# Moving the activation tiles by 192 bytes, and cutting 512-column products into halves, in a one-layer hybrid decoder kernel

## The chip, the cores and the metric

The kernel runs on one core of one Trainium2 chip. The metric is the time of one execution on the device in microseconds (us). Three runs of the kernel before gave 962.97, 963.48 and 963.52 us; the median, 963.48 us, is what the changed kernel is held against.

## The reference

One layer of a decoder trunk in float32, on 512 positions of width 1024. What matters here is the list of matrix products and what stands between them:

```
h    = rmsnorm(x, norm_mix_g)
proj = h @ w_in                          # 1024 x 9232
bg, cg, xv, q, k, v, z, a, b, ga, gb = split(proj)
y_a  = (bg * causal_dwconv(cg * xv, conv_a_w)) @ w_a_out
y_b  = gdn_branch(q, k, v, z, a, b, ...) @ w_b_out   # chunked gated delta rule
mix  = sigmoid(ga) * y_a + sigmoid(gb) * y_b
x    = x + mix @ w_o
h    = rmsnorm(x, norm_ffn_g)
gate, val = split(causal_dwconv(h @ w_up, ffn_conv_w))   # 2 x 2816
x    = x + (silu(gate) * val) @ w_down
out  = rmsnorm(x, norm_final_g)
```

## The kernel before

**Products.** Activations are held transposed: 128 channels of a block on the partitions, the 512 positions in the free dimension. Every float32 operand is split into a rounded part and a remainder (`wh`, `wl` for weights, two tiles for activations), and a product of two of them is three TensorE products with rounded operands, all issued by the helper `mm` (line 108 of the profile). In a product one operand streams through the array (the moving one, 512 or 256 columns of it), the other is loaded into it beforehand by a weight load (the stationary one, 128 columns). Each product here has a weight load of its own.

**Jobs.** The program is a list of jobs, and each takes a block of weights (four quarter tiles `wh` and four `wl`, from 12 buffers of each). A *plain job* (`col_job`) makes 256 output channels: two banks, 24 products of 512 columns into each, 48 in all. A *sum job* (`sum_job`) makes the same output by a Strassen-like scheme from 84 products of 256 columns: 12 on a quarter of the activations, 48 on sums of quarters (tiles `ts` for the first norm's output `hT`, `us` for the second's, `h2`), and 24 on two more quarters. In both the weights are stationary and the activations move. In the `w_o` and `w_down` jobs the roles are exchanged: tiles `mix`, `mixb`, `xs` are stationary, and `wh`, `wl` move, 512 columns nearly always.

**Stages.** To about 29 us: the first norm and the first K job, partly by an order written out by hand (`manual_schedule`). Then 19 plain jobs on `hT` (Q, V, Z, K of four head pairs, and the gate GB), and between their products the small float32 products of the delta rule (to about 314 us). Then 16 jobs for CG, XV, BG and GA (ten sum jobs, six plain), four plain jobs each on `yas` and `yb`, the `w_o` jobs on `mix` and `mixb` (to about 613 us), the second norm, the 22 jobs of `w_up` (eight sum jobs on `h2` and `us`; two blocks at the start that already go by halves of 256 columns, lines 1440 to 1460; twelve plain), and the `w_down` jobs on `xs`.

**What sets the order.** `mm` counts columns, and after every `SLAB * S` = 2048 of them (four products of 512 columns, or eight of 256) it calls `tick`, which advances the side work by a step: the delta rule's chains, the evacuation of a finished bank (`evacs`, always only the task at the head of the queue), the splitting of the next block of weights (`splits`: `act.copy` line 140, `dve.tensor_tensor` line 141). On top of the order in which the program issues things, the framework's scheduler places instructions on each engine by its own costs, outside the hand-ordered stretches. A finished bank of a Q, K or V job goes through `conv` in a tile `cv` (three buffers) and a Silu (line 973).

**Where tiles lie.** The addresses are fixed when the program is built. Per partition, modulo 256 bytes, the tiles start at:

| tile | before | after | start minus that of `wh`, before | after |
|---|---|---|---|---|
| `wh`, `wl`, `raw` | 32 | 224 | 0 | 0 |
| `hT`, `h2` | 32 | 160 | 0 | 192 |
| `ts`, `us` | 224 | 160 | 192 | 192 |
| `yas` | 96 | 224 | 64 | 0 |
| `yb` | 32 | 224 | 0 | 0 |
| `mix`, `mixb`, `xs` | 224 | 224 | 192 | 0 |

All slices of them that a product reads start a multiple of 256 bytes further. Below, the fourth and fifth columns are called the *offset* of an operand pair. The small float32 products of the delta rule read tiles that all move by the same amount, so their offsets stay.

Of the kernel before, what the change touches and what calls it, by code (L numbers as in the profile page):

```python
# [9 lines left out]
F32 = mybir.dt.float32  # L10
F32R = mybir.dt.float32r
# [5 lines left out]
P = 128  # L17
S = 512
NT = S // P
D = 1024  # L20
ND = D // P
# [39 lines left out]
def layer_kernel(ctx, tc, x, norm_mix_g, w_in, w_ab, conv_a_w, gdn_conv_w, gdn_A_log, gdn_dt_bias,  # L61
# [14 lines left out]
    def nm(s):  # L76
        cnt[0] += 1
        return f"{s}{cnt[0]}"
# [137 lines left out]
            use(block.wh, block.wl)  # L216


    gate = const.tile([1, 16], F32, name="gate")

    def feed(raw):
        el = raw[0:1, 1].rearrange("p k n -> p (k n)") if len(raw.shape) == 4 else raw[0:1, 1]
# [8 lines left out]
    def products(o, wh, wl, j, x_, lo=0, hi=S, order=KO):  # L231
        mm3(o[:, lo:hi], [(piece(wh, j, k), piece(wl, j, k), x_[0][:, k, lo:hi], x_[1][:, k, lo:hi])
                          for k in order])

    def col_job(w, i, xs, consume, pre=None):
        def use(wh, wl):
            if pre:
                pre()
            x_ = xs() if callable(xs) else xs
            for j in range(GW // P):  # L240
                o = bank()
                products(o, wh, wl, j, x_)
                evacs.append(Task(consume(j, o)))
        return Block(lambda: w[i]), use

# [24 lines left out]
    def sum_job(w, i, xs, sums, consume, place, pre=None):  # L270
# [56 lines left out]
            evacs.append(Task(last()))  # L327
        return SumBlock(lambda: w[i]), use

    def split(dst, idx, src):  # L330
        act.copy(out=dst[0][:, idx], in_=src)
        dve.tensor_tensor(out=dst[1][:, idx], in0=src, in1=dst[0][:, idx].bitcast(F32), op=ALU.subtract)
# [26 lines left out]

    p1 = ExitStack()  # L360
    hp = p1.enter_context(tc.tile_pool(name="hp", bufs=1))
    hT = [hp.tile([P, ND, S], F32R, tag=f"h{i}", name=f"hT{i}") for i in range(2)]
    yb = hp.tile([P, ND, S], F32, name="yb")


# [15 lines left out]
    HS = S // 2  # L381
# [227 lines left out]
    Dms = {}  # L609

    def gates_chain(o):
        abT = gd.tile([P, S], F32, tag="cv", bufs=3, name="abT")[0:32]
        act.copy(out=abT, in_=o[0:32, :])
        yield
        o2 = bank()
# [342 lines left out]
    def pair_jobs(pr):  # L958
        st = {}

        def qkv(which, j, o):
            c = gd.tile([P, S], F32, tag="cv", bufs=3, name=nm("cv"))
            yield from conv(c, o, gdn_w(which * 8 + 2 * pr + j), 4)
            if which == 1 and j == 0:
                reach(pr - 2, 99)
                st["kq"] = gd.tile([P, 2, 2, S], F32, tag="kq", bufs=2, name=nm("kq"))
                st["kqs"] = hp.tile([P, 2, 2, 2, S], F32R, tag="s", name=nm("kqs"))
            if which == 2 and j == 0:
                if pr:
                    ftask[pr - 1].until(VREAD)  # L970
                st["vT"] = gd.tile([P, 2, S], F32, tag="vT", name=nm("vT"))
            dst = (lambda: st["kq"][:, j, 1, :], lambda: st["kq"][:, j, 0, :], lambda: st["vT"][:, j, :])[which]()
            act.activation(out=dst, in_=c, func=AF.Silu)
            yield
            if which < 2:
                hi, lo = (st["kqs"][:, i, j, 1 - which, :] for i in range(2))
                act.copy(out=hi, in_=dst)
                dve.tensor_tensor(out=lo, in0=dst, in1=hi.bitcast(F32), op=ALU.subtract)
                yield
            if which == 2 and j == 1:  # L980
                st["v"] = True
            if which == 0 and j == 1:
                ftask[pr] = Task(front(pr, st))
                chains.append(ftask[pr])

        def zc(j, o):
            act.activation(out=yb[:, 2 * pr + j, :], in_=o, func=AF.Silu)
            if j == 1:
                st["z"] = True
            yield  # L990

        def first_k(wh, wl):
            use_ab()
            for j in range(2):
                products(o_k[j], wh, wl, j, hT, HS, S)
                evacs.append(Task(qkv(1, j, o_k[j])))

        return [(k_block, first_k) if pr == 0 else col_job(w_in, C_K + pr, hT, lambda j, o: qkv(1, j, o)),
                col_job(w_in, C_Q + pr, hT, lambda j, o: qkv(0, j, o)),
                col_job(w_in, C_V + pr, hT, lambda j, o: qkv(2, j, o)),  # L1000
                col_job(w_in, C_Z + pr, hT, zc)]
# [21 lines left out]
    st = {}  # L1023
# [52 lines left out]
    def open_conv():  # L1076
        drain(evacs)
        drain(chains)
        drain(mids)
        drain(backs)  # L1080
        p2.close()
        sc = st["sc"] = p3.enter_context(tc.tile_pool(name="sc", bufs=1, side="right"))
        st["ts"] = [place(i, "ts").rearrange("p (m a n) -> p m a n", m=4, a=4) for i in range(2)]
        st["ya"] = sc.tile([P, ND, S], F32, name="ya")
        room["pool"] = sc
        adds.extend((Task(o_w.form()), Task(down_w.form())))
        sums_of.append(Task(activation_sums(hT, st["ts"], sc.tile([P, ND, S], F32, tag="mixa", name="xf"))))


    def place(i, name, up=0):  # L1090
        return st["sc"].tile([P, ND * S + 64], F32R, tag=f"t{i}", name=f"{name}{i}")[:, up:up + ND * S]

    def open_mix():
        st["mixa"] = st["sc"].tile([P, ND, S], F32, tag="mixa", name="mixa")
# [65 lines left out]
        return c  # L1160

    def split_ya():
        st["yas"] = [place(i, "yas", 32).rearrange("p (k n) -> p k n", k=ND) for i in range(2)]
        for k in range(ND):
            split(st["yas"], k, st["ya"][:, k, :])
            yield

    def split_yb():
        st["yb"] = [hp.tile([P, ND, S], F32R, tag=f"h{i}", name=f"yb{i}") for i in range(2)]
        for k in range(ND):  # L1170
            split(st["yb"], k, yb[:, k, :])
            yield
# [18 lines left out]
    def wb_c(g):  # L1191
        def c(j, o):
            m = 2 * g + j
            t, mix = tmp("t"), st["mixa"][:, m, :]
            dve.tensor_tensor(out=t, in0=o, in1=sgb[0][:, m, :], op=ALU.mult)
            dve.tensor_tensor(out=mix, in0=t, in1=mix, op=ALU.add)
            yield
            if j == 1 and g % 2 == 1:
                if g == 1:
                    st["mix"] = [place(i, "mix").rearrange("p (m a n) -> p m a n", m=4, a=4) for i in range(2)]  # L1200
                yield from prep_a(mix_pairs(g - 1), st["mix"], g - 1)
        return c

# [93 lines left out]
    def open_o():  # L1297
# [2 lines left out]
        fp = ctx.enter_context(tc.tile_pool(name="fp", bufs=1))  # L1300
        st["x1"] = fp.tile([P, NT, D], F32, name="x1")
        st["fp"] = fp
        st["h2"] = [fp.tile([P, ND, S], F32R, tag=f"h2{i}", name=f"h2{i}") for i in range(2)]
        s7 = st["s7"] = p7.enter_context(tc.tile_pool(name="s7", bufs=2))
        gff = st["gff"] = s7.tile([P, D], F32, name="gff", bufs=1)
        nc.sync.dma_start(out=gff, in_=norm_ffn_g[0].partition_broadcast(P))
# [85 lines left out]
    def open_up():  # L1392
# [2 lines left out]
        up = st["up"] = ctx.enter_context(tc.tile_pool(name="up", bufs=1, side="right"))  # L1395
        cvp = st["cvp"] = ctx.enter_context(tc.tile_pool(name="cvp", bufs=2))
        room["pool"], room["o"] = cvp, 2
        st["ts"] = [up.tile([P, 4, 4, HS], F32R, tag=f"t{i}", name=f"us{i}") for i in range(2)]
        st["aT"] = [up.tile([P, NA, S], F32, name="aTa")]
        xf = up.tile([P, ND, S], F32, tag="late", name="xf2")  # L1400
        st["gfn"] = cvp.tile([P, D], F32, name="gfn", bufs=1)
# [66 lines left out]

    def xs():
        if "xs" not in st:  # L1470
            st["xs"] = [st["up"].tile([P, 4, 4, HS], F32R, tag=f"t{e}", name=f"xs{e}") for e in range(2)]
        return st["xs"]

    def ffn_pairs(g, n):
# [206 lines left out]
```

## Time and profile before

| what | value |
|---|---|
| median of three runs | 963.48 us |
| the profiled execution's own time | 963.13 us |
| its span, first to last instruction | 961.4 us |
| TensorE (PE) busy | 950.7 us, 99% |
| VectorE (DVE) busy | 743.9 us, 77% |
| ScalarE (ACT) busy | 507.6 us, 53% |
| DMA | 138.11 MB, mean 144 GB/s |
| granted TensorE clock | 0.998 |

A row of the timeline gives the start of a run of like instructions, the time to the end of its last one, engine, line, operation, `out<-in` by tile names, and the number merged into the row. Matmuls are pipelined: the next starts long before the one before it has ended, so the *spacing*, from start to start, is what a product costs, and not its duration.

### The profile page before, as it was taken

The page shows a single profiled execution, that of the slowest core. Times are in us where ns is not written, and L with a number is a line of the kernel's source. Part 1 is how long each engine was busy: PE and PEld are TensorE (multiplying, and loading weights), DVE is VectorE, ACT ScalarE, POOL GpSimd, SP SyncE. Part 2 cuts the span into 40 slices and gives each one's busy share as a digit, 9 for nine tenths or more (in the row PEclk, how much of TensorE's full clock was granted, in tenths as well). Part 3 has the DMA queues.
Part 4 walks back from the last instruction along what each step waited for, and adds up shares of the span by engine and source line. Part 5 has one row for each costly group of instructions (what it writes and reads, how often), then busy time and mean ns, then how long its engine had stood idle before and what let it go on. Part 6 is the DMA issues. An engine that isn't in the chain of part 4 may idle for free.

```text
span 961.4 us, 16188 instructions
## 1 busy us (share of the span) xinstructions
PE 950.7 (99%) x6188; PEld 823.1 (86%) x6188; DVE 743.9 (77%) x1401; ACT 507.6 (53%) x1073; POOL 155.6 (16%) x251
## 2 busy tenths in 40 slices
PE   8999999999999999999999999999999999999997
PEld 7888887987878889999988888998889999888885
DVE  6878686896725958799873479999988888969775
ACT  7895556565444434344651235645645456556463
POOL 3430300202000212312222100232222210000000
PEclk9999999999999999999999999999999999999999
DMA  6544312223121456667788435584775673176232
GB/s 227 157 137 123 94 53 89 75 57 93 53 89 45 144 130 140 175 162 170 215 270 174 120 112 217 152 231 162 177 191 180 185 160 132 45 264 228 100 132 88
DMA packets 51629, 138.11 MB, mean 144 GB/s; under 512 B 21691, under 2 KB 22112, under 8 KB 42848
## 3 DMA queue, kind: packets, MB, share of 16 engines
q1 hardware_dynamic: 38864, 107.45, 32.7%
q0 software_dynamic: 12544, 29.37, 16.1%
q8 instruction: 48, 0.79, 0.3%
q14 instruction: 29, 0.24, 0.1%
q10 hardware_dynamic: 144, 0.26, 0.1%
HBM read 133.64 MB, written 32.78 MB: 173 GB/s over the span
## 4 chain that ended last, share of the span: by engine, by line
PE 91%; DVE 4%; ACT 1%; issue 1%; POOL 1%; POOLq 0%
PE ps L108 83%; PE ps L689 1%; PE ps L724 1%; DVE wl L141 1%; PE ps L898 1%; PE ps L918 1%; DVE hn L1325 1%; DVE h L1339 1%; PE ps L907 1%; PE ps L886 0%; PE ps L885 0%; PE ps L862 0%; PE ps L856 0%; POOL r L1323 0%; PE ps L800 0%
## 5 line engine op out<-in xcount | busy, mean ns | idle before, releaser
L108 PE MATMUL ps<-hT,wh 128*128 128x512 f32 (+1 forms) x1104 | 318.1, 368 | 0.3 <-DVE hT L509 0.3
L140 ACT CAST wh<-raw 128x512 fp32r<-128x512 f32 x350 | 203.6, 619 | 217.0 <-PE ps L108 143.5
L141 DVE TENSOR_TENSOR wl<-raw,wh 128x512 fp32r<-128x512 f32 x350 | 233.3, 692 | 61.2 <-ACT wh L140 60.3
L108 PEld LDWEIGHTS ps<-hT,wh 128*128 128x128 f32 x1104 | 196.6, 189 | 28.9 <-DVE hT L509 0.5
L108 PE MATMUL ps<-hT,wl 128*128 128x512 f32 (+1 forms) x552 | 195.0, 361 | 0.0
L108 PE MATMUL ps<-h,wh 128*128 128x512 f32 (+1 forms) x704 | 177.7, 341 | 0.3 <-DVE h L1339 0.3
L108 PEld LDWEIGHTS ps<-h,wh 128*128 128x128 f32 x704 | 122.3, 189 | 15.6 <-DVE h L1339 0.5
L108 PEld LDWEIGHTS ps<-hT,wl 128*128 128x128 f32 x552 | 104.3, 189 | 13.8
L108 PE MATMUL ps<-h,wl 128*128 128x512 f32 (+1 forms) x352 | 114.5, 341 | 0.0
L108 PE MATMUL ps<-wh,xs 128*128 128x512 f32 (+1 forms) x320 | 96.9, 384 | 0.0
L108 PEld LDWEIGHTS ps<-h,wl 128*128 128x128 f32 x352 | 66.6, 189 | 7.6
L108 PEld LDWEIGHTS ps<-wh,xs 128*128 128x128 f32 x320 | 59.6, 188 | 13.1
L108 PE MATMUL ps<-wl,xs 128*128 128x512 f32 (+1 forms) x160 | 62.1, 388 | 0.0
L223 POOL COPY gate<-raw 1x1 f32<-1x1 f32 x38 | 16.7, 441 | 268.3 <-DMA raw<-in_w_in_dram 120.5
L338 DVE SCALAR_TENSOR_TENSOR cv<-ps,wA,cv 128x511 f32<-128x511 f32 (+2 forms) x72 | 53.2, 742 | 4.1 <-ACT cv L335 3.9
L108 PE MATMUL ps<-ts,wh 128*128 128x256 f32 x320 | 56.2, 276 | 0.0
L140 ACT CAST wh<-raws 128x512 fp32r<-128x512 f32 x66 | 39.3, 620 | 26.7 <-PE ps L108 8.9
L141 DVE TENSOR_TENSOR wl<-raws,wh 128x512 fp32r<-128x512 f32 x66 | 42.9, 687 | 12.5 <-ACT wh L140 12.5
L161 DVE TENSOR_TENSOR raw<-raw 128x512 f32<-128x512 f32 x72 | 49.5, 687 | 1.4
L108 PEld LDWEIGHTS ps<-ts,wh 128*128 128x128 f32 x320 | 49.0, 188 | 0.0
L108 PE MATMUL ps<-us,wh 128*128 128x256 f32 x256 | 45.0, 276 | 0.0
L108 PE MATMUL ps<-yas,wh 128*128 128x512 f32 x128 | 39.9, 391 | 0.0
(316 smaller groups left out, 1550.6 us busy)
## 6 DMA issues: line engine op xcount, KB each, us to landing
raw<-in_w_in_dram SPq DMA_DIRECT2D x35, 1024.0 KB, 5.3
raw<-in_w_up_dram SPq DMA_DIRECT2D x22, 1024.0 KB, 5.2
dv<-in_w_down_dram POOLq DMA_DIRECT2D x50, 256.0 KB, 6.1
raws<-dv SPq DMA_DIRECT2D x8, 768.0 KB, 5.8
ov<-in_w_o_dram POOLq DMA_DIRECT2D x20, 256.0 KB, 5.2
raws<-in_w_down_dram SPq DMA_DIRECT2D x10, 512.0 KB, 6.0
raw<-in_w_a_out_dram SPq DMA_DIRECT2D x4, 1024.0 KB
raw<-in_w_b_out_dram SPq DMA_DIRECT2D x4, 1024.0 KB, 6.6
```

The lines of the kernel that those rows point to most:

```text
L108: pe.matmul(o, lhsT=a, rhs=b, start=start, stop=stop, skip_group_check=free)
L140: act.copy(out=wh, in_=src)
L141: dve.tensor_tensor(out=wl, in0=src, in1=wh.bitcast(F32), op=ALU.subtract)
L161: dve.tensor_tensor(out=r[q], in0=a, in1=b, op=op)
L223: tc.keep_in_program_order(pool.tensor_copy(out=gate[:, 0:1], in_=el[:, 0:1]))
L338: dve.scalar_tensor_tensor(out=dst[:, sh:], in0=src[:, :S - sh], scalar=wcol(j), in1=dst[:, sh:], op0=ALU.mult, op1=ALU.add)
L689: pe.transpose(out=o[:, n * P:(n + 1) * P], in_=src[:, n * P:(n + 1) * P], identity=ident)
L724: pe.matmul(o[:, i], lhsT=kqs[:, a, h, 0, sl], rhs=kqs[:, b, h, :, sl], start=a > 0, stop=a + b == 0)
L898: pe.matmul(o[:, 0:P], lhsT=TTf[:, f, :], rhs=rs[h], start=True, stop=True)
L907: pe.matmul(o2[:, 0:P], lhsT=kn[:, f, :], rhs=vns[h], start=True, stop=True)
L918: pe.matmul(o[:, 0:P], lhsT=A[:, f, :], rhs=vns[h], start=True, stop=True)
L1325: dve.scalar_tensor_tensor(out=hn_[:, sl], in0=x1[:, t, sl], scalar=r, in1=st["gff"][:, sl], op0=ALU.mult, op1=ALU.mult)
```

## The change

Three things. (1) A constant tile grows from 64 to 256 bytes, which moves all tiles behind it by 192 bytes; `place`, which adds 64 spare elements to a tile and starts its view some elements into it, is now used for `hT`, `yb`, `h2`, `us` and `xs` too, and `ts`, `us`, `hT` and `h2` start `UP` = 48 elements (192 bytes) in. To make room, `cv` has two buffers in place of three. (2) A plain job whose activations are `hT` or `h2` goes through each bank by two halves of 256 columns, with 24 products on each half: 96 products of 256 columns in place of 48 of 512, so twice the weight loads. Jobs on `yas` and `yb` keep 512 columns. (3) Since the scheduler places by its costs, some instructions take another place.

```diff
-    gate = const.tile([1, 16], F32, name="gate")
+    gate = const.tile([1, 64], F32, name="gate")
...
             for j in range(GW // P):
                 o = bank()
-                products(o, wh, wl, j, x_)
+                step = HS if x_ is hT or x_ is st.get("h2") else S
+                for lo in range(0, S, step):
+                    products(o, wh, wl, j, x_, lo, lo + step)
                 evacs.append(Task(consume(j, o)))
...
+    UP = 48
+
+    def place(pool_, tag, name, up=0):
+        t = pool_.tile([P, ND * S + 64], F32R, tag=tag, name=name)[:, up:up + ND * S]
+        return t.rearrange("p (m a n) -> p m a n", m=4, a=4)
+
+    def by_rows(t):
+        return t.rearrange("p m a n -> p (m a n)").rearrange("p (k n) -> p k n", k=ND)
...
-    hT = [hp.tile([P, ND, S], F32R, tag=f"h{i}", name=f"hT{i}") for i in range(2)]
+    hT = [by_rows(place(hp, f"h{i}", f"hT{i}", UP)) for i in range(2)]
...
-            c = gd.tile([P, S], F32, tag="cv", bufs=3, name=nm("cv"))
+            c = gd.tile([P, S], F32, tag="cv", bufs=2, name=nm("cv"))
...
-        st["ts"] = [place(i, "ts").rearrange("p (m a n) -> p m a n", m=4, a=4) for i in range(2)]
+        st["ts"] = [place(sc, f"t{i}", f"ts{i}", UP) for i in range(2)]
...
-        st["yas"] = [place(i, "yas", 32).rearrange("p (k n) -> p k n", k=ND) for i in range(2)]
+        st["yas"] = [by_rows(place(st["sc"], f"t{i}", f"yas{i}")) for i in range(2)]
...
-        st["yb"] = [hp.tile([P, ND, S], F32R, tag=f"h{i}", name=f"yb{i}") for i in range(2)]
+        st["yb"] = [by_rows(place(hp, f"h{i}", f"yb{i}")) for i in range(2)]
...
-        st["h2"] = [fp.tile([P, ND, S], F32R, tag=f"h2{i}", name=f"h2{i}") for i in range(2)]
+        st["h2"] = [by_rows(place(fp, f"h2{i}", f"h2{i}", UP)) for i in range(2)]
...
-        st["ts"] = [up.tile([P, 4, 4, HS], F32R, tag=f"t{i}", name=f"us{i}") for i in range(2)]
+        st["ts"] = [place(up, f"t{i}", f"us{i}", UP) for i in range(2)]
...
-            st["xs"] = [st["up"].tile([P, 4, 4, HS], F32R, tag=f"t{e}", name=f"xs{e}") for e in range(2)]
+            st["xs"] = [place(st["up"], f"t{e}", f"xs{e}") for e in range(2)]
```

Two places show what moves. The first is on PE, in the first Z job, around the transposes of `vT` (the V job's output; line 689 before, 701 after), which stand between the job's products. Before:

```order
L689 MATMUL ps_900<-ident,vT_769 128x128 x4
L108 MATMUL ps_895<-hT_82,wh_667 128x512
L108 MATMUL ps_895<-hT_81,wl_668 128x512
...
L108 MATMUL ps_895<-hT_81,wh_710 128x512 x2
L108 MATMUL ps_895<-hT_81,wh_667 128x512
L689 MATMUL ps_905<-ident,vT_769 128x128 x4
L108 MATMUL ps_895<-hT_81,wh_667 128x512
```

Of the change:

```order
L701 MATMUL ps_1024<-ident,vT_849 128x128 x4
L108 MATMUL ps_1015<-hT_82,wh_774 128x256
L108 MATMUL ps_1015<-hT_81,wl_775 128x256
...
L108 MATMUL ps_1015<-hT_81,wh_774 128x256 x2
L108 MATMUL ps_1015<-hT_81,wh_727 128x256 x2
L108 MATMUL ps_1015<-hT_81,wh_774 128x256
L701 MATMUL ps_1029<-ident,vT_849 128x128 x4
L108 MATMUL ps_1015<-hT_81,wh_774 128x256
```

The products go by 256 columns, and the second group of transposes, which stood 15 products of 512 columns behind the first, now stands 13 of 256 behind it.

The second is on SP, the queue that loads the weights (`raw`) and carries the small transfers of the delta rule's last head pair (`UB`, `tbd`, `T`). Before:

```order
L135 DMA raw_3315<-in_w_in_dram 128x2048
L740 DMA UB_2876<-ucd_97 32x16x16 x2
L135 DMA raw_3478<-in_w_in_dram 128x2048
L780 DMA tbd_101<-TB_2877 32x16x16 x2
L785 DMA T_3183<-tbd_101 32x8x32 x4
L135 DMA raw_3679<-in_w_in_dram 128x2048
```

Of the change:

```order
L752 DMA UB_3496<-ucd_97 32x16x16 x2
L135 DMA raw_4035<-in_w_in_dram 128x2048
L792 DMA tbd_101<-TB_3497 32x16x16 x2
L797 DMA T_3859<-tbd_101 32x8x32 x4
L135 DMA raw_4246<-in_w_in_dram 128x2048
L135 DMA raw_4495<-in_w_in_dram 128x2048
```

One weight load (`raw_3478` before, `raw_4246` after) now stands behind the six small transfers that it stood ahead of.

More of the change, by code (lines that the diff above doesn't have):

```diff
@@ L611, in gates_chain @@
     def gates_chain(o):
-        abT = gd.tile([P, S], F32, tag="cv", bufs=3, name="abT")[0:32]
+        abT = gd.tile([P, S], F32, tag="cv", bufs=2, name="abT")[0:32]
         act.copy(out=abT, in_=o[0:32, :])
@@ L1087, in open_conv @@
         sums_of.append(Task(activation_sums(hT, st["ts"], sc.tile([P, ND, S], F32, tag="mixa", name="xf"))))
-    def place(i, name, up=0):
-        return st["sc"].tile([P, ND * S + 64], F32R, tag=f"t{i}", name=f"{name}{i}")[:, up:up + ND * S]
     def open_mix():
@@ L1199, in c @@
                 if g == 1:
-                    st["mix"] = [place(i, "mix").rearrange("p (m a n) -> p m a n", m=4, a=4) for i in range(2)]
+                    st["mix"] = [place(st["sc"], f"t{i}", f"mix{i}") for i in range(2)]
                 yield from prep_a(mix_pairs(g - 1), st["mix"], g - 1)
```

## The prediction

> **What bounds the kernel now.** I read the page's busy table and its chain first, then the waits of TensorE.
>
> ```profile
> PE 950.7 (99%) x6188; PEld 823.1 (86%) x6188; DVE 743.9 (77%) x1401; ACT 507.6 (53%) x1073; POOL 155.6 (16%) x251
> PE 91%; DVE 4%; ACT 1%; issue 1%; POOL 1%; POOLq 0%
> PE ps L689 <- DVE vs L937: 0.5, 1, 0.5
> ```
>
> PE is busy for 99% of the span and has 91% of the chain. After the first 30 us its waits are this one of 0.5 us and one of 0.3 us, which stands in a row below. So the time is the sum of the spacings of PE's products, and the question is what one costs. The groups by shape count those concerned:
>
> ```profile
> L108 PE MATMUL ps<-hT,wh 128*128 128x512 f32 x800 | 260.4, 400 | 0.0
> L108 PE MATMUL ps<-hT,wl 128*128 128x512 f32 x400 | 156.6, 392 | 0.0
> L108 PE MATMUL ps<-h,wh 128*128 128x512 f32 x384 | 119.8, 389 | 0.0
> L108 PE MATMUL ps<-h,wl 128*128 128x512 f32 x192 | 74.8, 390 | 0.0
> L108 PE MATMUL ps<-h,wh 128*128 128x256 f32 x320 | 60.7, 284 | 0.3 <-DVE h L1339 0.3
> L108 PE MATMUL ps<-h,wl 128*128 128x256 f32 x160 | 39.7, 282 | 0.0
> L108 PE MATMUL ps<-hT,wh 128*128 128x256 f32 x304 | 58.9, 284 | 0.3 <-DVE hT L509 0.3
> L108 PE MATMUL ps<-hT,wl 128*128 128x256 f32 x152 | 38.4, 282 | 0.0
> ```
>
> Their mean durations overlap and say little; the spacing does. In a stretch of like products the timeline merges the last, equal ones of an accumulation into one row, so from such a row to the next is a whole accumulation: 12 products in a sum job, 24 in a plain one.
>
> ```profile
> 378.96 0.73 PE L108 MATMUL ps<-ts,wh 128*128 128x256 f32 x5
> 380.32 0.73 PE L108 MATMUL ps<-ts,wh 128*128 128x256 f32 x5
> ...
> 383.07 0.76 PE L108 MATMUL ps<-hT,wh 128*128 128x256 f32 x5
> 384.51 0.76 PE L108 MATMUL ps<-hT,wh 128*128 128x256 f32 x5
> ...
> 693.96 2.20 PE L108 MATMUL ps<-h,wh 128*128 128x512 f32 x9
> 699.40 2.09 PE L108 MATMUL ps<-h,wh 128*128 128x512 f32 x9
> ...
> 488.56 2.22 PE L108 MATMUL ps<-yas,wh 128*128 128x512 f32 x9
> 494.05 2.22 PE L108 MATMUL ps<-yas,wh 128*128 128x512 f32 x9
> ...
> 537.96 2.20 PE L108 MATMUL ps<-yb,wh 128*128 128x512 f32 x9
> 543.40 2.20 PE L108 MATMUL ps<-yb,wh 128*128 128x512 f32 x9
> ...
> 900.26 0.62 PE L108 MATMUL ps<-wh,xs 128*128 128x512 f32 x2
> 901.64 0.62 PE L108 MATMUL ps<-wh,xs 128*128 128x512 f32 x2
> ```
>
> - `ts`, 256 columns, offset 192: 1.36 / 12 = 113.3 ns.
> - `hT`, 256 columns, offset 0: 1.44 / 12 = 120.0 ns, in the same job.
> - `h`, 512 columns, offset 0: 5.44 / 24 = 226.7 ns.
> - `yb`, 512 columns, offset 0: 226.7 ns; `yas`, the same job and layout at offset 64: 5.49 / 24 = 228.8 ns.
> - `xs`, 512 columns with the roles exchanged: 1.38 / 6 = 230 ns.
>
> `yb` against `yas` is the cleanest pair: only the place differs, and the spacing with it. From 256 to 512 columns at offset 0 is 106.7 ns, so a product there is its columns at 106.7 ns per 256 and 13.3 ns more; at offset 192 the 256-column one carries 6.7 ns more. Two halves at offset 192 (2 x 113.3 = 226.7) cost what one product of 512 costs at offset 0, to the last digit.
>
> **The change part by part.**
>
> *(a) Halves at offset 0 become halves at offset 192.* These are the 304 + 152 of `hT` and the 320 + 160 of `h`. In the sum jobs they are 10 x 36 and 8 x 36 = 648 (a job has 84, 48 of them on `ts` or `us`). Now 120.0 each, less a little in the first few of a group; I take 6.0 ns saved: 648 x 6.0 = 3.9 us. The other halves of `h`, 192 of them, stand in the first two blocks of `w_up`:
>
> ```profile
> 592.50:627.40 34.90, 34.64 (x217) 30.70 (x216) 33.38 (x60) 18.60 (x40) 5.95 (x8) 1.00 0.46 139
> 627.44 0.39 PE L108 MATMUL ps<-h,wh 128*128 128x256 f32 x1 [0.31 <-DVE h L1339]
> ```
>
> The window's columns are its length, then PE, PEld, DVE, ACT and POOL busy. DVE is full for 33.4 of 34.9 us, and PE waits at the end for the `h` that DVE writes last. What PE gains from 592 to 627 (112 halves, 0.75 us, and some 0.2 us of (c)) makes that wait longer and nothing shorter: 0. The 80 left give 0.5 us. The first K job's 96 stand before 29 us; its last 48 flow freely: 0.3 us; the rest follows ACT and DVE: 0. In all 4.7 us.
>
> *(b) Plain jobs.* 800 + 400 + 384 + 192 = 1776 products of 512 become 3552 of 256 with as many weight loads. By the row of `ts`: 1776 x (2 x 113.3 - 226.7) = 0. That row is the nearest, being the same operation at the same offset in the same kind of stream, and I take it; bounds are below. What is gained is at the seams:
>
> ```profile
> 690.54 0.40 PE L108 MATMUL ps<-h,wl 128*128 128x512 f32 x1
> ...
> 661.32:666.78 5.46, 5.46 (x50) 1.00 0.76 221
> ```
>
> From this product, the second of a plain job behind a sum job, to the 17th at 693.96 are 15 in 3.42 us, 0.02 over 15 x 226.7. And the window holds the 48 products of a `us` stretch, 0.02 over 48 x 113.3 (its count takes in neighbours that reach over the edges). With all spacings alike both go: some 12 plain seams and 18 stretches, 0.6 us.
>
> *(c) `yas`, `xs`, `mix` to offset 0.* `yas`: 192 x 2.1 = 0.4 us. `xs`: 456 products of 512, 230 to 226.7 at most, and its whole stretch averages
>
> ```profile
> 846.93:951.30 104.37, 104.37 (x457) 1.00 0.48 168
> ```
>
> 228.9 ns, so 456 x 2.2 = 1.0 us. `mix` before 592 us, 88 products: 0.2 us. The row for offset 0 has the activations moving; here the weights move. Bounds: 1.6 us down, and nothing gained at the other end; I take 1.6, by `yb`.
>
> *(d) Between the delta rule's products.* To 314 us PE leaves the plain jobs 91 times for small float32 products (the first and the last such restart are the first and third row here). What follows a restart has a spacing of its own:
>
> ```profile
> 43.15 0.48 PE L108 MATMUL ps<-hT,wh 128*128 128x512 f32 x1
> ...
> 44.16 0.27 PE L665 MATMUL ps<-ident,G 128*32 128x128 f32 x1
> ...
> 313.68 0.48 PE L108 MATMUL ps<-hT,wh 128*128 128x512 f32 x1
> ...
> 617.00 0.36 PE L108 MATMUL ps<-h,wh 128*128 128x256 f32 x1
> 618.03 0.60 PE L1334 MATMUL ps<-ident,hn 128*128 128x128 f32 x4
> ```
>
> From 43.15 to 44.16 us are four products of 512: 1.01 us, where a steady stream has 0.907. From 617.00 to 618.03 are eight halves at offset 0: 1.03 us, 0.07 over their steady 0.96. At offset 192 no row shows a restart. Bounds: the halves' full 1.03 (+0.02 x 91 = +1.8 us), or 0.907 + 0.07 = 0.98 (-0.03 x 91 = -2.7 us). I take +0: the first products after a break looked alike at both widths.
>
> *(e) What the scheduler moved.* The second `vT` transposes come on PE 13 halves after the first:
>
> ```profile
> 62.60 0.60 PE L689 MATMUL ps<-ident,vT 128*128 128x128 f32 x4
> 64.89 0.65 ACT L973 ACTIVATE vT<-cv 128x512 f32<-128x512 f32 x1
> ```
>
> 62.60 + 0.36 + 13 x 0.115 = 64.5 us, and ACT ended that `vT` at 65.5. Behind PE's wait stand the rest of the Z job and all that follows, so it counts in full: 1.0 us if ACT is no earlier, 0 if it is; I take 0.3. The weight load that moves behind SP's small transfers is issued late by
>
> ```profile
> 249.15 0.35 SPq L135 DMA_DIRECT2D raw<-in_w_in_dram  x1
> 256.09 1.78 SPq L785 DMA_DIRECT2D T<-tbd  x4
> 268.42 0.62 ACT L140 CAST wh<-raw 128x512 fp32r<-128x512 f32 x1 [4.71 <-PE ps L108]
> ...
> raw<-in_w_in_dram SPq DMA_DIRECT2D x35, 1024.0 KB, 5.3
> ```
>
> some 8.8 us, at 257.9. Its first reader, the cast at 268.42, waited for PE and not for it. These loads land 5.3 us after issue, at 263 us: 5 us of cover, so 0; without it, ACT would be late, and PE only when three blocks of finished weights are used up. `cv` with two buffers: only the head task of `evacs` runs, and a buffer's last reader, a Silu, is ahead of its next writer on ACT itself: 0.
>
> Sum: 4.7 + 0.6 + 1.6 - 0.3 = 6.6 us off the profiled 963.13 us (its span 961.4 and 1.7 around it): 956.5. That run is 0.35 below the median, so the **forecast is 956.9 us** against 963.48.
>
> **Who takes over.** Half a per cent is little for the other engines to keep up with, except DVE here:
>
> ```profile
> 675.00:700.00 25.00, 25.00 (x153) 22.37 (x152) 24.18 (x39) 14.09 (x25) 5.39 (x8) 1.00 0.74 177
> ```
>
> DVE is busy for 24.18 of 25 us, 96.7%. A gate and value pair there (36 x 120.0 + 48 x 113.3 + 48 x 226.7 = 20.64 us) gets 0.26 us shorter, 1.3%, so DVE would have 98%: it fits, and I take no cost.
>
> **Rivals.**
>
> *Slower: the start of a product costs the same wherever its operands lie.* Then the 113.3 of `ts` is not its offset but its layout (its rows of a product lie 1024 bytes apart, those of `hT` 2048), the halves of the plain jobs cost 120.0, and each of 1776 pairs is 13.3 ns dearer: +23.6 us, with nothing from (a), (b) and (c): 987 us. The point from which it decides: over 115 ns for a half, (b) has eaten the rest (1776 x 2 x 1.9 = 6.7 us). For it: `ts` and `hT` differ in both. Against it: `yas` and `yb` differ in place alone, and 228.8 is not 226.7. [...] Chance 0.10.
>
> *The gain is eaten on the way.* DVE becomes the bound in the `w_up` stage (2.0 us of (a) and (b) lost), the restarts cost their upper bound (1.8), the `vT` wait its full 1.0: 956.9 + 2.0 + 1.8 + 0.7 = 961.4 us. For it: 24.18 of 25. Against it: PE never waited for DVE there. Chance 0.17, a third of it within 0.2% of before.
>
> *The new order makes PE wait.* The delta rule's chain runs through DVE, DMA and ACT, and PE takes its products in a fixed order; if more of them stand too early, each costs a microsecond or so, as `vs` did (0.5). Eight such waits would be 964 us. Chance 0.04, and slower from ten.
>
> **How the numbers follow.** The forecast has 0.69, and its own range is 955 to 959. A measurement of this kernel can tell 0.2%, 1.9 us, from no change. Faster: 0.69 + 0.11 = 0.80; same: 0.06 from the eaten gain and 0.01 from the waits, 0.07; slower: 0.10 + 0.03 = 0.13. The range: down by the restarts (2.7) and the part before 627 us that I gave to DVE (1.0), to 953.2; up to the eaten gain, 961.5.
>
> **What would show it.** `hT` and `h` halves 12 apart by 1.36 us in sum jobs and 24 apart by 2.72 in plain ones (2.88 is the first rival). `yas` at 5.44 per 24, `xs` at 1.36 per 6. After a break, eight halves in 0.98 to 1.03 us. PE's wait for DVE's `h` near 622 us longer by about a microsecond. No PE wait for `vT` over a microsecond, none between 640 and 830 us. I am wrong if a half in a plain job keeps 115 ns or more, or if PE's waits grow by several microseconds.

## The result: 0.98% slower

The changed kernel took 972.86 us (median of four executions, 971.46 to 975.28), the kernel before 963.50 us beside it (962.97 to 964.00). The ratio is 1.0098, 95% interval 1.0085 to 1.0112. The forecast was 956.9 us, and its range, 953.2 to 961.5, misses the time by 11 us. The profiled execution took 973.04 us with a span of 971.4, 10.0 more than before.

The busy table and the chain of its page:

```profile
PE 958.5 (99%) x7964; PEld 908.3 (94%) x7964; DVE 743.6 (77%) x1401; ACT 502.8 (52%) x1071; POOL 151.8 (16%) x251
PE 89%; DVE 4%; DMA 1%; ACT 1%; issue 1%; POOL 1%; POOLq 0%; DVEq 0%; ACTq 0%
```

And the longest wait of TensorE in the answer on waits (us in total, times, longest):

```profile
PE ps L108 <- DVE kn L722: 1.9, 1, 1.9
```

PE is busy all the time, as before, and for 8 us longer. So its products have become dearer. The timeline's merged rows of plain jobs on `hT` (24 halves from one to the next) and of `ts` (12) say where:

```profile
320.62 1.22 PE L108 MATMUL ps<-hT,wh 128*128 128x256 f32 x9
323.44 1.22 PE L108 MATMUL ps<-hT,wh 128*128 128x256 f32 x9
...
363.49 0.75 PE L108 MATMUL ps<-ts,wh 128*128 128x256 f32 x5
364.90 0.75 PE L108 MATMUL ps<-ts,wh 128*128 128x256 f32 x5
...
415.37 0.73 PE L108 MATMUL ps<-ts,wh 128*128 128x256 f32 x5
416.73 0.73 PE L108 MATMUL ps<-ts,wh 128*128 128x256 f32 x5
...
481.56 1.18 PE L108 MATMUL ps<-hT,wh 128*128 128x256 f32 x9
484.28 1.18 PE L108 MATMUL ps<-hT,wh 128*128 128x256 f32 x9
```

`hT` at 320 us: 2.82 / 24 = 117.5 ns. `hT` at 481 us: 2.72 / 24 = 113.3. The same tiles, the same operation, the same offset, and two spacings. `ts` has both as well: 1.41 / 12 = 117.5 and 1.36 / 12 = 113.3. From the starts in the trace the two are 117.78 and 113.33 ns, and nothing lies between them for long: from the last restart to 400.6 us all is slow, from there to 490 us fast, from 633 to 858 us slow, 1911 halves without a break. I call them the *slow* and the *fast* spacing. The windows of the last two plain jobs of `w_up` (312 halves) and of the `w_down` stage:

```profile
821.04:857.78 36.74, 36.74 (x314) 36.74 (x313) 32.57 (x46) 17.15 (x27) 0.00 (x0) 1.00 0.16 58
857.78:961.17 103.39, 103.39 (x459) 85.63 (x457) 80.95 (x123) 58.65 (x99) 0.56 (x1) 1.00 0.49 171
```

36.74 / 312 = 117.8 ns at a granted clock of 1.00; and `xs` takes 103.39 us where it took 104.37.

How far the changed kernel is behind, at the product that has as many columns of products ahead of it in both (worked out from the starts in the two traces):

| at, in the kernel before | reached | behind by |
|---|---|---|
| 29 us | end of the first K job | 0.6 us |
| 56 us | in the V job | 2.8 us |
| 310 us | end of the delta rule | 4.9 us |
| 395 us | in the sum jobs on `hT` | 7.5 us |
| 485 us | first job on `yas` | 5.8 us |
| 613 us | first job on `h` | 5.1 us |
| 847 us | first job on `xs` | 10.9 us |
| 952 us | near the end | 9.9 us |

Summed over the gaps between halves up to 130 ns, what lies over 113.33 ns is 4.7 us from 56 to 310 us, 3.2 us to 395, nothing to 485, and 8.1 us from 638 to 847 (times of the kernel before, as in the table): 16.0 us.

### The profile page after: what moved, and what is told of

Same layout as the page of the kernel before. It is cut to its first block, busy times and chain, and to the rows that moved or that the text cites. A ratio compares the mean times of both kernels' runs of the same rounds, so it can differ in the third digit from the quotient of the medians.

```text
span 971.4 us, 19732 instructions
## 1 busy us (share of the span) xinstructions
PE 958.5 (99%) x7964; PEld 908.3 (94%) x7964; DVE 743.6 (77%) x1401; ACT 502.8 (52%) x1071; POOL 151.8 (16%) x251
## 4 chain that ended last, share of the span: by engine, by line
PE 89%; DVE 4%; DMA 1%; ACT 1%; issue 1%; POOL 1%; POOLq 0%; DVEq 0%; ACTq 0%
PE ps L108 82%; PE ps L701 1%; DVE wl L141 1%; PE ps L736 1%; PE ps L930 1%; PE ps L910 1%; DMA Dm<-gtd 1%; PE ps L898 1%; PE ps L919 1%; PE ps L897 1%; DMA raw<-in_w_in_dram 1%; DVE h L1347 0%; DVE hn L1333 0%; PE ps L874 0%; PE ps L868 0%
## 5 line engine op out<-in xcount | busy, mean ns | idle before, releaser
L108 PE MATMUL ps<-hT,wh 128*128 128x256 f32 x1904 | 351.0, 283 | 2.2 <-DVE kn L722 1.9
L108 PEld LDWEIGHTS ps<-hT,wh 128*128 128x128 f32 x1904 | 294.1, 189 | 3.9 <-DVE kn L722 2.2
L108 PE MATMUL ps<-hT,wl 128*128 128x256 f32 x952 | 230.0, 279 | 0.0
L108 PE MATMUL ps<-h,wh 128*128 128x256 f32 x1088 | 194.1, 281 | 0.7 <-DVE h L1347 0.7
L108 PEld LDWEIGHTS ps<-hT,wl 128*128 128x128 f32 x952 | 179.7, 189 | 0.0
L108 PEld LDWEIGHTS ps<-h,wh 128*128 128x128 f32 x1088 | 167.4, 189 | 0.9 <-DVE h L1347 0.9
L108 PE MATMUL ps<-h,wl 128*128 128x256 f32 x544 | 131.8, 281 | 0.0
L108 PEld LDWEIGHTS ps<-h,wl 128*128 128x128 f32 x544 | 103.0, 189 | 0.0
L1066 POOL DMA_DIRECT2D dv<-in_w_down_dram x50 | 36.1, 794 | 25.3 <-issue 25.1
```

The lines of the kernel that those rows point to most:

```text
L108: pe.matmul(o, lhsT=a, rhs=b, start=start, stop=stop, skip_group_check=free)
L1066: tc.keep_in_program_order(pool.dma_start(out=self.at(g, to), in_=src, **kw))
```

## The experiments

Theory A was that a stream of halves at offset 192 has two steady spacings, and keeps the one in which it was entered. Theory B: the place is worth nothing and the cut costs. Theory C: the two `cv` buffers, the scheduler's order or the other engines cost it.

**Plain jobs uncut, at offset 192.**

```diff
-                step = HS if x_ is hT or x_ is st.get("h2") else S
+                step = S
```

> The changed kernel with its plain jobs on hT and h uncut, 512 columns, at offset 192. Theory A (at offset 192 a stream of halves has two steady spacings, 113.3 and 117.8 ns, and which one it has depends on how it was entered): the cut is what costs, since 1776 pairs now run mostly at 2 x 117.8 = 235.6; a whole product there carries 6.7 to 11.1 ns over its columns, 220.0 to 224.4 ns, so 4 to 12 us below the kernel before in the plain jobs, and about 948 to 960 us in all. Theory B (the place is worth nothing and the cut costs by itself): 963.5. Theory C (two cv buffers and the scheduler's new order cost the time): 970 or more, since both stay.

Measured: 965.93 us, ratio 1.0026 (1.0016 to 1.0035). From one merged row of a plain job to the next:

```profile
323.44 2.27 PE L108 MATMUL ps<-hT,wh 128*128 128x512 f32 x9
329.04 2.27 PE L108 MATMUL ps<-hT,wh 128*128 128x512 f32 x9
```

5.60 / 24 = 233.3 ns. A's 220 to 224 was wrong, and so was its time; B's 963.5 is 2.4 us short. A whole product at offset 192 is dearer than one at offset 0 (226.7), where a half in the fast spacing is cheaper than one at offset 0 (113.3 against 120.0). What a place costs is not a constant beside the columns. Against the same kernel at offset 0 (962.10 us, two runs further down) moving `hT` and `h2` to offset 192 costs 3.8 us in all, and the cut then adds 6.9. The profiled execution, 969.21 us, was the slowest of ten. By the starts in it, the halves of the sum jobs on `hT` are slow throughout (117.8 ns) and those of the sum jobs in `w_up` fast (113.3), though both stages enter them from whole products at offset 192.

**Halves, but `hT` and `h2` at offset 0.**

```diff
-    hT = [by_rows(place(hp, f"h{i}", f"hT{i}", UP)) for i in range(2)]
+    hT = [by_rows(place(hp, f"h{i}", f"hT{i}")) for i in range(2)]
...
-        st["h2"] = [by_rows(place(fp, f"h2{i}", f"h2{i}", UP)) for i in range(2)]
+        st["h2"] = [by_rows(place(fp, f"h2{i}", f"h2{i}")) for i in range(2)]
```

> The changed kernel, still cut into halves, with hT and h2 back at offset 0 (ts and us stay at 192). Theory A: the halves of hT and h have one spacing, 120.0 ns, so 1776 pairs x 13.3 = 23.6 us over whole products; with -1.6 us from yas, xs and mix and some -2 us at the restarts, 982 to 987 us. Theory B: a half costs the same in either place, so as the changed kernel, 972.9. Theory C: 972.9 as well.

Measured: 983.98 us, ratio 1.0214 (1.0190 to 1.0238).

```profile
331.10 1.24 PE L108 MATMUL ps<-hT,wh 128*128 128x256 f32 x9
333.98 1.24 PE L108 MATMUL ps<-hT,wh 128*128 128x256 f32 x9
```

2.88 / 24 = 120.0 ns, as theory A has it: the place is worth 11 us here, and B falls.

**Both undone: what is left is `yas`, `xs`, `mix` at offset 0, two `cv` buffers and the common move.** (The edits of the last two together.)

> hT and h2 at offset 0 and uncut; what stays of the change is yas, xs and mix at offset 0, cv with two buffers, and the tiles' common move. Theory A: 963.5 - 1.6 = 961.9 us, with xs and yas at 226.7 ns. Theory B: 963.5 less the 1.6 us that the changed kernel's trace shows. Theory C: 970 or more, since the cv buffers and a new order of the scheduler stay.

Measured: 962.10 us (961.46 to 962.37), ratio 0.9980 (0.9971 to 0.9990): faster than both kernels, and 0.2 us from what A gave. One row of `xs` to the next is three products:

```profile
900.35 0.62 PE L108 MATMUL ps<-wh,xs 128*128 128x512 f32 x2
901.03 0.62 PE L108 MATMUL ps<-wh,xs 128*128 128x512 f32 x2
```

0.68 / 3 = 226.7 ns. Theory C's 970 falls: two `cv` buffers cost nothing.

**The streams alone.** A kernel of products only: eight moving tiles `xa` to `xh` at offsets 0, 32, ... 224 (`xg` is 192), each entered in several ways.

```python
rest()                        # four small float32 products
halves(c + "brk", i)          # 192 halves
rest()
whole(c + "whl", i, 1)        # 24 products of 512
halves(c + "aftw", i, 2)      # 96 halves behind them
whole("z", 0, 1)              # offset 0
halves(c + "aftzw", i, 2)
rest()
halves("z", 0, 1)             # halves at offset 0
halves(c + "aftzh", i, 2)
```

> Not the layer: x is copied to the output and the layer is left out; streams of products with the moving tile at offsets 0, 32, 64, ... 224 from the stationary one, as halves behind a break of four small float32 products, as whole products, and as halves behind whole products at the same offset, behind whole products at offset 0, and behind halves at offset 0. Theory A: at offset 192 halves go at 113.3 or 117.8 ns by the entry: 113.3 behind halves at offset 0, 117.8 behind a break; at offset 0 120.0 in every entry, whole products 226.7. Theory B: one spacing at every offset and entry. No expectation for the offsets not used so far, but that 64 has whole products at 228.8.

Rows of its timeline, for offset 0, 64 (`xc`) and 192; where a group starts directly behind another, the difference of the starts is the whole group:

```profile
66.36 11.68 PE L95 MATMUL aaftw<-xa,wt 128*128 128x256 f32 x96
77.88 5.63 PE L95 MATMUL z<-xa,wt 128*128 128x512 f32 x24
...
218.56 11.04 PE L95 MATMUL caftw<-xc,wt 128*128 128x256 f32 x96
229.44 5.63 PE L95 MATMUL z<-xa,wt 128*128 128x512 f32 x24
234.90 11.47 PE L95 MATMUL caftzw<-xc,wt 128*128 128x256 f32 x96
...
523.22 11.47 PE L95 MATMUL gaftw<-xg,wt 128*128 128x256 f32 x96
534.53 5.62 PE L95 MATMUL z<-xa,wt 128*128 128x512 f32 x24
539.99 11.47 PE L95 MATMUL gaftzw<-xg,wt 128*128 128x256 f32 x96
...
557.94 11.06 PE L95 MATMUL gaftzh<-xg,wt 128*128 128x256 f32 x96
```

At offset 0: (77.88 - 66.36) / 96 = 120.0 ns. At 192 behind whole products: 11.31 / 96 = 117.8; behind halves at offset 0 the row is 0.41 us shorter than that, 96 x 4.3 ns: the fast spacing. Offset 64 has the same two, 10.88 / 96 = 113.3 behind whole products at 64 and 117.8 behind those at 0. This is theory A without another engine at work, and without `hT`, `ts` or a scheduler. One part of it missed: behind a break the stream at 192 was fast here (113.3 ns), where 117.8 was expected. The streams also explain the kernel before: there `ts` and `us` are always entered from twelve halves at offset 0, and behind eight or more of them every stream at 192 was fast, in this kernel of streams and in the two below.

Behind a break the same instructions took 113.3 ns at offset 192 and 120.0 at offset 0, by the place alone. What in the chip makes it so, no run shows.

**Finer places.** The same streams at offsets between; the table has both kernels (ns per product; a steady value from the starts).

> Not the layer: its work is left out. The same streams with the moving tile at finer offsets: 16, 48, 56, 64, 72, 80, 144, 176 to 208, 240 bytes; halves behind a break, behind whole products and behind halves at offset 0, and whole products behind a break. Theory A (two operands read at places that meet modulo some block): spacings change in steps of a block, 32 or 64 bytes, and within a block are equal; an offset with 113.3 ns from all three entries may be among them. Theory B: one spacing for all.

| offset | halves, behind a break | behind whole at 0 | behind halves at 0 | whole |
|---|---|---|---|---|
| 0 | 120.0 | 120.0 | 120.0 | 226.7 |
| 32 | 116.7 | 116.7 | 117.8 | 233.3 |
| 64 | 117.8 | 117.8 | 117.8 | 228.9 |
| 96 | 120.0 | 120.0 | 120.0 | 233.3 |
| 128 | 118.7 | 120.0 | 118.7 | 232.4 |
| 188 | 115.6 | 120.0 | 120.0 | 230.8 |
| 192 | 113.3, 117.8 | 117.8 | 113.3 | 233.3 |
| 196 | 120.0 | 120.0 | 120.0 | 240.0 |
| 224 | 118.3 | 118.3 | 118.3 | 233.3 |

The expectation of steps of 32 or 64 bytes was wrong: 4 bytes beside 192 the fast spacing is gone. No place in the table has 113.3 from every entry, and none has whole products under 226.7. Behind a break the two kernels of streams found different spacings at 192 (113.3 in the first, 117.8 in this one).

**Switching the spacing.** 32 halves at 192 entered from eight whole products (`s`, meant to be slow) or 16 halves at offset 0 (`f`, meant to be fast), a disturbance, 48 more (`post`). All 23 `f` streams came in fast; of the 23 `s` streams, 19 came in slow and four fast, so whole products at offset 0 are no sure entry to the slow spacing.

> Not the layer: its work is left out. Streams of halves at offset 192, brought into the slower spacing (behind whole products at offset 0, 117.8 ns) or the faster one (behind halves at offset 0, 113.3 ns); then one disturbance, then 48 more halves. Disturbances: none; one half cut in two; one product of 32 to 192 columns more; one to eight halves at offset 0; one half at another offset; one whole product at 192; one small float32 product. Theory A: with none the spacing stays what it was; some disturbances switch it, as the gaps of 147 and 223 ns at 400.6 us of the changed kernel did; eight halves at offset 0 give 113.3 from either. Theory B: the spacing comes back to one value after any disturbance.

```profile
41.45 5.82 PE L95 MATMUL snonepost<-xg,wt 128*128 128x256 f32 x48
...
52.66 5.60 PE L95 MATMUL fnonepost<-xg,wt 128*128 128x256 f32 x48
...
108.73 0.33 PE L123 MATMUL cut<-xg,wt 128*128 128x128 f32 x2
108.90 5.68 PE L95 MATMUL scutcpost<-xg,wt 128*128 128x256 f32 x48
...
120.14 5.67 PE L95 MATMUL fcutcpost<-xg,wt 128*128 128x256 f32 x48
...
165.11 5.90 PE L95 MATMUL faddapost<-xg,wt 128*128 128x256 f32 x48
```

Undisturbed, 48 halves last 5.82 us or 5.60, as they came. One half cut into 128 + 128 columns leaves both at 5.67 to 5.68, the fast one and some 0.08 us of settling; so did all four ways of cutting, from either spacing, for about 0.14 us in all. One more product of 32 columns (`adda`) turned the fast spacing into the slow one. Two halves at offset 0 turned each into the other, eight gave the fast one from both, and so did one small float32 product, six times of six. So theory B's one value is wrong: the spacing is switched by what comes between, not by the tiles.

**The cut in the layer.** One half cut in two jobs, then in four.

```diff
+KNOCK = (20, 53)        # the second kernel: (4, 12, 20, 53)
...
-            mm(o, al, bh, False, False, free)
+            if knock[0]:
+                knock[0] = False
+                for part in (slice(0, 128), slice(128, HS)):
+                    mm(o[:, part], al, bh[:, part], False, False, free)
+            else:
+                mm(o, al, bh, False, False, free)
...
+            knock[0] = i in KNOCK
             use(block.wh, block.wl)
```

> The changed kernel, with one half of one accumulation cut into 128 + 128 columns at two places: in the first XV job behind the delta rule (at about 327 us) and in the first plain job of w_up behind its two opening blocks (at about 643 us). In the streams alone such a cut cost about 0.14 us and put them into 113.3 ns from either spacing. Theory A: from 327 to 401 us (some 630 halves) and from 643 to 858 us (some 1825) the spacing falls from 117.8 to 113.3: 2.8 + 8.1 - 0.3 = 10.6 us, so 962 us; elsewhere as the changed kernel. Theory B (the cut into halves or the scheduler's order costs by itself, whatever the spacing's state): 973.1, two more instructions. Theory C (the slow spacing comes from what other engines do in these stages): the stream falls back to 117.8 within some microseconds, 970 or more.

> As the run with two cuts, and two more in the delta rule's stage, in the jobs that begin at about 71 and 202 us of the changed kernel. Theory A: some 230 and 125 halves, until PE next leaves the stream, go at 113.3: 1.0 + 0.6 - 0.3 = 1.3 us less than with two cuts, about 961 us. Theory B: as the changed kernel, 973. Theory C: no gain from the two added cuts, as with two.

Measured: two cuts 971.52 us (967.14 to 973.58), ratio 1.0072 (1.0046 to 1.0097); four cuts 967.08 (961.59 to 972.34), ratio 1.0031 (1.0007 to 1.0055). The profiled execution with two cuts took 968.38. Its timeline ahead of the first cut and at it, and then what made PE stop at 400 us:

```profile
323.53 1.22 PE L110 MATMUL ps<-hT,wh 128*128 128x256 f32 x9
326.36 1.22 PE L110 MATMUL ps<-hT,wh 128*128 128x256 f32 x9
327.42 0.33 PE L110 MATMUL ps<-hT,wl 128*128 128x128 f32 x2
...
383.80 2.52 POOL L1076 DMA_DIRECT2D ov<-in_w_o_dram  x3
386.48 0.33 SPq L144 DMA_DIRECT2D raw<-in_w_in_dram  x1
396.72 1.15 ACT L149 CAST wh<-raw 128x512 fp32r<-128x512 f32 x2 [6.14 <-DMA raw<-in_w_in_dram]
401.30 0.39 PE L110 MATMUL ps<-hT,wh 128*128 128x256 f32 x1 [2.97 <-DVE u L305]
```

The two windows below (columns: length, PE, PEld, DVE, ACT, POOL busy, the granted clock, DMA share, GB/s) are the one behind that stop and the last 312 halves of `w_up`:

```profile
402.00:405.00 3.00, 3.00 (x17) 3.00 (x16) 3.00 (x7) 0.80 (x3) 0.15 (x1) 0.50 0.78 296
817.75:853.12 35.37, 35.37 (x315) 35.37 (x314) 32.83 (x46) 17.21 (x28) 0.00 (x0) 1.00 0.19 61
```

Ahead of the first cut it is 2.83 / 24 = 117.9 ns; behind it, by the starts, 113.4 over 620 halves up to 398 us. The fast spacing came with the cut and held, and C's "it falls back" is wrong. In the profiled executions of the four kernels with cuts (two here, two below) eight streams were slow ahead of a cut, and all eight were fast behind it; six were fast already and stayed so. The cut in `w_up`, at 644.89 us, is one of these six:

```profile
638.43 1.18 PE L110 MATMUL ps<-h,wh 128*128 128x256 f32 x9
641.15 1.18 PE L110 MATMUL ps<-h,wh 128*128 128x256 f32 x9
```

2.72 / 24 = 113.3 ns ahead of it, as 35.37 / 312 = 113.4 at the end. In `w_up` the stream had become fast at its restart behind the wait for `h` (634.7 us), so the 8 us there are not the work of the cut. The same holds for the other three kernels with cuts.

By the time alone two cuts are not told from the changed kernel: 1.0072 and 1.0098, and the intervals meet; four cuts are. The executions lie up to 11 us apart, and only the profiled ones can be explained. In the one with two cuts 6 us of A's 10.6 went elsewhere. In the fast spacing the sum jobs catch up with their weight loads: the load issued at 386.48 us has its first packet at 390.5, when 0.66 of the 0.79 MB of the three `ov` transfers that GpSimd issued from 383.80 have been moved. ACT waits 6.14 us for weights, DVE's `u` comes late behind that, and PE stands for 2.97 us. Behind the stop the granted clock is 0.50 (first window), for 3.4 us in all, which by an estimate from these two numbers, half of 3.4 us, costs 1.7 us more; with 4.1 us of waits for `u` in all, that is the 6 us.

Behind this stop of 2.97 us the half clock lasted 3.41 us. Behind shorter stops it came only sometimes: in the four-cut kernel the clock was 0.50 from 60.0 us for 3.41 us, behind a wait of 1.9 us for `kn`, and stayed at 1.00 behind one of 2.1 us for `u`; behind the 1.9 us wait of the changed kernel it stayed at 1.00.

**Thinner weight-sum transfers.** With the four cuts, and, as a control, without them:

```diff
-                feed(jobs[i + 2][0].raw)
+                feed(jobs[i + 2][0].raw, 2 if i <= 30 or 53 <= i <= 57 else 4 if 35 <= i <= 41 else FEED)
```

> The run with four cuts, and GpSimd issues its transfers that form weight sums in DRAM (the tiles ov and dv) more thinly where the first sum jobs stand: two per job instead of three in jobs 20 to 30 and 53 to 57, four in jobs 35 to 41. In the four-cut run PE waited 3.6 us for DVE's u, behind a weight load whose first packet came 4 us after its issue, when three such transfers had ended; behind a wait the granted clock was 0.50 for some 3 us. Theory A (the fast spacing leaves the weight loads no slack against these transfers): the waits for u shrink to under 1 us, the executions lie closer together, and the time falls by 3.6 us and the half clock's 3 us or so, to about 960 us. Theory B (the waits come from ACT's and DVE's own order): no change, 967.

> The changed kernel with the thinner issue of the weight-sum transfers alone, and no cuts. Theory A: at 117.8 ns PE waits for no load (0.1 us at 400.6 us), so nothing is gained, 972 to 973 us; if that small wait goes, so does the switch to 113.3 ns behind it, and the stretch from 401 to 490 us stays at 117.8: +3.5 us, 976. Theory B: 972.9.

Measured: with the cuts 963.50 us (961.89 to 969.07), ratio 1.0005 (0.9992 to 1.0018); without them 974.70 (970.77 to 976.78), ratio 1.0112 (1.0090 to 1.0133). The waits for `u` with four cuts, and then with the thinner transfers besides:

```profile
PE ps L110 <- DVE u L305: 3.6, 2, 2.1
```

```profile
PE ps L110 <- DVE u L305: 0.8, 1, 0.8
```

The waits shrink, as A had it, but the median falls by 3.6 us and not by the 7 that A added up, and the two intervals meet. One term was mis-sized: 3.4 us at half the clock cost 1.7 us, by the estimate above, and not 3, and in the profiled four-cut execution they stood behind the wait for `kn`, which this edit leaves. Where the rest is, these runs don't tell.

The two kernels with thinner transfers differ in the four cut halves alone: 974.70 us without them, 963.50 with them, 11.2 us, with the intervals well apart. In the profiled executions the halves behind 56 us take 19.1 and 3.9 us over 113.33 ns; some 8 us of this difference is `w_up`, which the restart made slow in the one and fast in the other. By the time alone the control is not told from the changed kernel (1.0112 and 1.0098), but its trace says the same the other way: without the small wait at 400.6 us its stream was not switched and stayed slow to the end of the `hT` jobs:

```profile
483.37 1.22 PE L108 MATMUL ps<-hT,wh 128*128 128x256 f32 x9
486.20 1.22 PE L108 MATMUL ps<-hT,wh 128*128 128x256 f32 x9
```

2.83 / 24 where the changed kernel had 2.72 / 24. In the changed kernel the stream became fast behind a wait of 0.1 us, and the 790 halves to 490 us took 3.5 us less for it.

**The wait for `kn`.** In the changed kernel:

```profile
55.51 2.45 ACT L618 ACTIVATE Dm<-Dm,negG 128x128 f32<-128x128 f32 x8 [1.98 <-POOL Dm L610]
57.86 0.25 ACT L721 ACTIVATE junk<-ps 128x128 f32<-128x128 f32 x1
...
58.24 0.69 DVE L722 TENSOR_TENSOR kn<-ps,kdv 128x512 f32<-128x512 f32 x1 [3.72 <-ACT junk L721]
...
58.99 0.38 PE L108 MATMUL ps<-hT,wh 128*128 128x256 f32 x1 [1.93 <-DVE kn L722]
```

The scheduler put eight exponentials, which wait for GpSimd's mask, ahead of the last of eight squares. The kernel with cuts and thinner transfers has this too; here they are issued behind the squares:

```diff
-        if pr == 0:
-            exps(0)
...
             yield
+        if pr == 0:
+            exps(0)
         dve.tensor_scalar(sk, ssk, EPS, None, op0=ALU.add)
```

> As the run with four cuts and thinner weight-sum transfers; besides, the eight exponentials Dm of the first head pair are issued behind the squares junk of the same chain, where the scheduler had put them ahead of the last one. In that run PE waited 2.1 us at about 57 us for DVE's kn, which waited for that square, and the eight exponentials took 2.5 us ahead of it, 2 us of ACT's idle time before them. Theory A: the wait was the order on ACT; it goes, and the time falls by 1.9 to 2.1 us, 963.5 to about 961.5 us. Theory B: the chain is late anyway, and the wait comes back at the products that need Dm or vT: 963 us or more.

Measured: 961.86 us (960.87 to 968.19), ratio 0.9992 (0.9979 to 1.0005). That is not clear of the 1.0005 (0.9992 to 1.0018) without this edit, so a gain in time is not shown. In the trace the wait for `kn` is gone, and part of it came back, as B had it, at a transpose of `vT`:

```profile
PE ps L711 <- ACT vT L996: 1.1, 1, 1.1
```

Its median is the lowest of all, but three of its twelve executions lie over 963 us. The better kernel is the third one: 962.10 us, 0.9980 of the kernel before beside it, with all ten executions within 0.9 us.

## Why the prediction was wrong

**(b) is the step that failed**: "1776 x (2 x 113.3 - 226.7) = 0. That row is the nearest, being the same operation at the same offset in the same kind of stream, and I take it". It was not the same kind of stream. In the kernel before, `ts` and `us` always follow halves at offset 0, which gave the fast spacing each time; a plain job at offset 192 follows a break or itself, and has either. Of 82 restarts of the changed kernel that begin with a gap over 195 ns and run for seven products or more, 41 settled slow within seven, 29 fast, 12 were still on the way. The point of decision, 115 ns, was placed rightly, and 117.8 lies beyond it; but the only way past it that I saw was the first rival's 120.0, which no run shows at offset 192 as the steady spacing of a stream. The range had no bound for the price of a half in another entry, though no row showed one. What the halves take over 113.33 ns is the 16.0 us above.

The gap between the first two products of a stream goes with the outcome: of the streams from 40 us on with 15 halves or more, all 15 with a gap of 220 to 223 ns became fast, and 9 of 10 with 200 or 201 ns and all three with 226 ns slow. The restart in `w_up` had 226 ns in the changed kernel and in the control without cuts, and was slow; it had 221 to 223 ns in the four kernels with cuts, and was fast. No run changed the gap alone, so whether it is the cause or a sign is not shown.

**(a)** falls with it: 648 halves were to save 6 ns each, and in the slow spacing save 2.2. In the fast stretch the term holds: seven sum jobs from 395 to 485 us gained 1.7 us, 0.24 each, which is 36 x 6.7 ns. What the first rival rested on, one cost of a product's start wherever its operands lie, does not agree with the runs: a half takes 113.3 or 117.8 ns at offset 192, by its entry, and 120.0 at offset 0, which is 6.7 to 13.3 ns beside its columns (106.7 ns, an estimate from the prediction's rows, 226.7 - 120.0).

**(c)** was right: `yas` and `mix` 0.7 us, `xs` 104.37 to 103.39, 1.0 us, at 226.7 ns throughout; alone, 1.8 us off the median.

**(d)** was right in its bounds and wrong in the value. Eight halves behind a break:

```profile
246.17 0.37 PE L108 MATMUL ps<-hT,wh 128*128 128x256 f32 x1
...
247.20 0.39 PE L897 MATMUL ps<-S,kq 128*128 128x128 f32 x2
...
248.01 0.36 PE L108 MATMUL ps<-hT,wh 128*128 128x256 f32 x1
...
249.01 0.60 PE L910 MATMUL ps<-r,TTf 128*128 128x128 f32 x4
```

1.03 us in the slow spacing, 1.00 in the fast one, where four whole products had taken 1.01. From 56 to 310 us the kernel fell behind by 2.1 us with 4.7 us of slow halves in it, so all else in the stage gained about 2.6 us. By these rows a restart in the fast spacing gains 0.01 us, 0.9 us for 91 of them; where the other 1.7 us of the stage come from is not shown.

**(e)** looked for waits on `vT` and on SP's loads; neither cost. What it missed was ACT's own queue: the exponentials ahead of the last square, 1.9 us. I had compared PE and SP, not ACT.

The sum, against the span of before: -4.4 ((a) and the seams: what the stages from 310 us on changed by, slow halves taken off, -0.6 - 1.7 - 2.1; the last from 640 us, where it was 4.9 us behind) - 1.7 (c) - 2.6 (the delta rule's stage, (d)) + 16.0 (slow spacing) + 1.9 (`kn`) + 0.6 (a later start, which from one of these kernels to the next was -0.3 to 0.7) = +9.8; measured 10.0. The rival of DVE as the bound in `w_up` did not come about: the changed kernel went through a pair there in 21.20 us, but the kernels with cuts in 20.40, and DVE kept up, but for one wait of 0.8 to 2.1 us for `u` near 670 us, behind a weight load. "The new order makes PE wait" was right in kind, with one wait in place of ten.

Open: what makes a break lead to one spacing or the other, what in the chip the two are, and what sets the executions of the kernels with cuts up to 11 us apart.

## What to carry to other kernels

A spacing read from one context is the spacing of that context: before it is used for 1776 other products, look at how the row's stream was entered, and measure the operation alone, in each entry that the new program has. A place of operands that is best for one width can be bad for another (192: 113.3 or 117.8 against 120.0 for 256 columns, 233.3 against 226.7 for 512). And when PE speeds up, look at the loads of the stage: with the halves 4% faster, PE stood for 3 us behind one weight load.

## What the runs showed of the hardware

- In the two kernels of streams with the moving tile at several places, the spacing of products went by the distance of the two operands' starts modulo 256 bytes, down to 4 bytes: for 256 columns from 113.3 ns (at 192) to 120.0 (at 0, and at 196), for 512 from 226.7 (at 0) to 240.0 (at 196).
- At distances of 64 and 192 bytes a stream of 256-column products had two steady spacings, 113.3 and 117.8 ns (113.33 and 117.78 at 192, in the changed kernel). It kept the one it had, for 1911 products once, over tiles and accumulations, until a gap, another width or another distance came between. One half cut in two gave the fast one from either, eight times of eight alone and fourteen of fourteen in the layer. At some other distances, too, the spacing went by the entry (116.7 and 117.8 at 32 bytes).
- A weight load that SP issued while three transfers of GpSimd were in flight had its first packet 4.0 us later (386.48 and 390.51), where it is 1.0 us for the load issued at 361.64 us. With two such transfers per job PE's waits behind these loads fell from 3.6 to 0.8 us.
- After a stop of 3.0 us the granted clock was 0.50 for 3.4 us. After a stop of 1.9 us it stayed at 1.00 in the changed kernel and was 0.50 for 3.4 us in the four-cut one; after one of 2.1 us it stayed at 1.00.
